# One layer's two seams: the first attention group prepared inside the projection, and the merge's first operands brought in under attention

## The chip, the cores and the metric

One core of a Trainium2 chip runs the whole program. The time is the device time of one execution in microseconds (us); of several runs the median is taken. The engines are TensorE (PE; its weight loads are listed as PEld), VectorE (DVE), ScalarE (ACT), GpSimd (POOL) and SyncE (SP), which here only issues transfers. POOL issues some transfers as well. Sums land in PSUM, whose regions carry names that begin with acc (accA, accS, accT, accO, accX, accC); everything else lies in SBUF.

## The reference

Two layers over 1024 latent tokens and, in the first layer only, 256 context tokens, all of width 1024. Each layer has a mixer (Fourier, global attention, window attention, gated merge) and an expert layer. The change touches the mixer.

```python
def mixer_sublayer(h, hc, cos, sin, w_in, ..., w_out, need_ctx):
    lf, lgq, lgk, lgv, lwq, lwk, lwv, lgate = split_proj(h @ w_in)
    cf, cgq, cgk, cgv, cwq, cwk, cwv, cgate = split_proj(hc @ w_in)
    ...
    o_g = global_attention(q_g, k_g, heads(lgv, G_KV), kc_g, vc_g)    # 8 heads, all keys
    ...
    o_w = window_attention(q_w, k_w, heads(lwv, W_KV), kc_w, vc_w, sink)   # 4 heads, band of 128 each way
    y = gated_merge(lgate, fourier_mix(lf), o_g, o_w,
                    w_br_fourier, w_br_global, w_br_window, w_out)

def gated_merge(gate_cols, f_mix, o_g, o_w, w_br_fourier, w_br_global, w_br_window, w_out):
    g = jax.nn.sigmoid(gate_cols).reshape(gate_cols.shape[:-1] + (N_BRANCH, D_MODEL))
    m = (g[..., 0, :] * (f_mix @ w_br_fourier)
         + g[..., 1, :] * (o_g @ w_br_global)
         + g[..., 2, :] * (o_w @ w_br_window))
    return m @ w_out
```

## The kernel before

Every product that needs full precision is done as three matmuls on a high and a low part of both operands (the helper `mm3`, lines 246 to 248 in the profile). The parts are made by a cast on ACT (line 229, for weights) and a subtraction on DVE (line 233).

A layer's mixer runs in four stages, one behind the other.

- `project` for the context and then for the latents: column blocks 0, 1 and 2 of `w_in`, each over eight tiles of 128 tokens, 24 matmuls of 128x512 a tile. `qtile` takes each finished tile out of PSUM: rotary products on DVE (lines 471 and 473) and POOL (477), the values V copied by ACT into `VT` (545). Block 2 is the last, and its eight tiles give the window heads' queries, keys and values.
- `attention`: 128 queries by four heads make a group. Groups of type 0 (global) have ten key tiles, those of type 1 (banded) four or five, and in the first layer there are groups of context queries with two. `build_k` turns the keys of one type: ten transposes by the identity, casts of the high part, subtractions for the low part. Of each group `prep` transposes the queries, `smax` multiplies the queries by all keys once to find row maxima (12 matmuls into the three banks accS in a group of type 0), `rmax` reduces these on DVE, `mdiag` and `mrow` set the maxima up as a row. Then come the group's steps, one for each key tile: `scores` (two matmuls into accT), the exponential on ACT, and `pv` (into accO) three steps later. `outp` and `recip` write sums to DRAM through SP. The preparation of later groups is spread over the steps of the earlier ones by `pace`; the first group's stands ahead of all steps. All instructions of this stage go through `Pin`, which fixes their order on each engine to the order in which they are written, and all of them carry the line of that helper, 754.
- `merge` in chunks of 512 tokens: `stage` loads the normalised tokens' parts HH and HL (eight transfers on POOL's queue, lines 1072 and 1073), `loads` brings the attention's output in (1078, on SP), multiplies its rows by the reciprocal sums (1095 and 1096) and makes its two parts OH and OL (1097 and 1098). `gates` runs twelve pieces, each two gate products (48 matmuls), a sigmoid (1136) and two branch products. In the first layer the generator `ada`, which makes the modulation rows of both layers, runs along: weights loaded by SP (311), products on ACT (335), sums on POOL (340) and on DVE (342), totals by a cast on ACT (318), a subtraction on DVE (319) and a few matmuls (321 and 322).
- the expert layer, which the change does not touch.

Outside `Pin` the scheduler sets each engine's order. PSUM has two layouts, `cut_main` and `cut_attn`; the projection uses the first, attention the second. SBUF is laid out by hand: `O_K` holds the projected keys, `O_H` first the normalised tokens (`LH`, `LL`) and during attention the turned keys, the number in a name such as a35840 being a place in SBUF.

## Time and profile before

| | us |
|---|---|
| median of 3 runs | 4104.14 |
| the 3 runs | 4103.4 to 4107.11 |
| the profiled execution | 4101.36 |
| its span in the trace | 4099.5 |

| | busy, share of the span |
|---|---|
| TensorE matmuls | 3734.9 us, 91% |
| VectorE | 2813.0 us, 69% |
| ScalarE | 2022.1 us, 49% |
| GpSimd | 682.3 us, 17% |

The tables of stages below give, for a stretch from one time to another (us from the span's start), the busy time of each engine and in brackets the number of its instructions, then the granted TensorE clock (1.00 is 2.4 GHz, 0.50 is 1.2 GHz) and the share and rate of the transfers. In the first layer the projection ends at 261, attention at 667 and the merge's first two pieces at about 733; in the second layer the same three places are 2543, 2929 and 2972.

### The profile page before, as it was taken

To read this page: it belongs to the slowest core of one execution; us is meant where nothing else is said; L and a number is where in the kernel's file an instruction comes from. 1 tells how busy PE (TensorE), PEld (TensorE's weight loads), DVE (VectorE), ACT (ScalarE), POOL (GpSimd) and SP (SyncE) were. 2 spreads that over 40 slices of the span, in tenths; PEclk is the share of its full clock that TensorE was granted. 3 is DMA by queue.
4 is the path that set the end of the run, shared out by engine and by line. 5 is a ranking of instruction groups with operands and counts; after the bars stand their busy time and mean duration, and the time that the engine had idled before them with its cause. 6 is when DMAs were issued, how large, how long until landed. Compare 5 with 4: busy or idle time off the path is not lost.

```text
span 4099.5 us, 52368 instructions
## 1 busy us (share of the span) xinstructions
PE 3734.9 (91%) x19185; PEld 2962.7 (72%) x19185; DVE 2813.0 (69%) x4989; ACT 2022.1 (49%) x3169; POOL 682.3 (17%) x558
## 2 busy tenths in 40 slices
PE   7979998899988698999999888999999994999997
PEld 4756665688788687778888666565588884777775
DVE  5855556957658577877777686555345747899988
ACT  4225555534424365556666541555432331777775
POOL 0240003512302423351000014000000001001000
PEclk9989999999999799999999998999999997999999
DMA  7331004555564477777777642200324434999996
GB/s 246 130 59 56 11 13 145 177 175 192 182 200 160 162 250 260 239 253 251 258 252 247 200 152 42 73 15 10 109 95 162 161 117 170 336 375 376 380 376 239
DMA packets 498542, 749.06 MB, mean 183 GB/s; under 512 B 27088, under 2 KB 291536, under 8 KB 498026
## 3 DMA queue, kind: packets, MB, share of 16 engines
q1 hardware_dynamic: 461164, 654.14, 46.5%
q0 software_dynamic: 31936, 72.70, 7.1%
q10 hardware_dynamic: 5184, 18.88, 1.1%
q8 instruction: 151, 2.47, 0.2%
q14 instruction: 107, 0.88, 0.1%
HBM read 675.21 MB, written 70.52 MB: 182 GB/s over the span
## 4 chain that ended last, share of the span: by engine, by line
PE 55%; DVE 16%; issue 15%; DMA 8%; ACT 3%; POOL 3%; SPq 0%; POOLq 0%; ACTq 0%; DVEq 0%
PE accA L246 11%; PE accA L248 11%; PE accA L247 10%; PE accO L754 8%; PE accT L754 4%; DVE a_r L233 4%; PE accS L754 3%; PE accA L1478 2%; DMA a_f<-in_w_in_dram 2%; POOL a_f L754 2%; PE accA L1476 2%; ACT a_r L229 1%; DVE a_f L342 1%; DMA a_f<-in_w_ada_dram 1%; DMA a_f<-in_w_down_e_dram 1%
## 5 line engine op out<-in xcount | busy, mean ns | idle before, releaser
L233 DVE TENSOR_TENSOR a_r<-a_f,a_r 128x1024 fp32r<-128x1024 f32 (+1 forms) x1008 | 1215.5, 1225 | 419.3 <-ACT a_r L229 396.7
L229 ACT CAST a_r<-a_f 128x1024 fp32r<-128x1024 f32 (+1 forms) x1036 | 1042.0, 1028 | 681.4 <-DVE a_r L233 260.1
L246 PE MATMUL accA<-a_r,a_r 128*128 128x512 f32 (+1 forms) x3280 | 1221.5, 374 | 54.9 <-DVE t L1163 9.2
L247 PE MATMUL accA<-a_r,a_r 128*128 128x512 f32 (+1 forms) x3280 | 1213.8, 371 | 23.2 <-DVE a_r L233 19.0
L248 PE MATMUL accA<-a_r,a_r 128*128 128x512 f32 (+1 forms) x3280 | 1209.8, 370 | 22.1 <-POOL a_r L231 8.5
L246 PEld LDWEIGHTS accA<-a_r,a_r 128*128 128x128 f32 x3280 | 629.4, 192 | 197.9 <-issue 14.2
L248 PEld LDWEIGHTS accA<-a_r,a_r 128*128 128x128 f32 x3280 | 628.5, 192 | 134.1 <-DVE a_r L1375 9.9
L247 PEld LDWEIGHTS accA<-a_r,a_r 128*128 128x128 f32 x3280 | 629.7, 192 | 129.0 <-DVE a_r L233 28.1
L1478 PE MATMUL accA<-a_r,a_r 128*128 128x320 f32 x2048 | 540.9, 316 | 18.1 <-DVE a_f L1486 15.4
L1476 PE MATMUL accA<-a_r,a_r 128*128 128x256 f32 x1792 | 487.3, 284 | 0.0
L754 DVE TENSOR_REDUCE m<-accS 128x1 f32<-128x512 f32 (+2 forms) x536 | 287.3, 560 | 224.0 <-PE accS L754 220.6
L754 PE MATMUL accO<-a_f,a_f 128*65 128x512 f32 (+1 forms) x976 | 416.0, 522 | 0.0
L754 PE MATMUL accT<-a_r,a_r 128*128 128x512 f32 (+1 forms) x976 | 404.0, 508 | 0.0
L754 ACT ACTIVATE a_f<-accT 128x512 f32<-128x512 f32 x408 | 243.7, 598 | 309.6 <-PE accT L754 307.1
L1478 PEld LDWEIGHTS accA<-a_r,a_r 128*128 128x128 f32 x2048 | 375.7, 192 | 21.9 <-DVE a_f L1486 17.1
L1476 PEld LDWEIGHTS accA<-a_r,a_r 128*128 128x128 f32 x1792 | 347.8, 194 | 0.7
L754 PEld LDWEIGHTS accT<-a_r,a_r 128*128 128x128 f32 x976 | 174.7, 191 | 181.2 <-issue 146.4
L754 PE MATMUL accS<-a_r,a_r 128*128 128x512 f32 (+2 forms) x704 | 208.8, 368 | 30.9 <-DVE a_r L754 19.3
L754 PEld LDWEIGHTS accS<-a_r,a_r 128*128 128x128 f32 x704 | 130.2, 202 | 64.3 <-DVE m L754 20.9
L754 PEld LDWEIGHTS accO<-a_f,a_f 128*65 128x65 f32 x976 | 127.0, 137 | 40.7 <-ACT a_f L754 0.3
L340 POOL TENSOR_TENSOR a_f<-a_f,a_f 128x512 f32<-128x512 f32 x84 | 136.0, 1620 | 104.9 <-ACT a_f L335 94.8
L1136 ACT ACTIVATE a_f<-accA 128x512 f32<-128x512 f32 (+1 forms) x120 | 66.2, 553 | 175.2 <-PE accA L248 174.3
(294 smaller groups left out, 3865.0 us busy)
## 6 DMA issues: line engine op xcount, KB each, us to landing
a_f<-in_w_gate_e_dram SPq DMA_DIRECT2D x128, 1024.0 KB
a_f<-in_w_up_e_dram SPq DMA_DIRECT2D x128, 1024.0 KB
a_f<-in_w_down_e_dram SPq DMA_DIRECT2D x128, 1024.0 KB
a_f<-in_w_in_dram SPq DMA_DIRECT2D x60, 1024.0 KB
a_f<-in_w_ada_dram SPq DMA_DIRECT2D x60, 512.0 KB
a_f<-in_w_out_dram SPq DMA_DIRECT2D x20, 1024.0 KB
a_f<-in_w_in_dram SPq DMA_DIRECT2D x36, 512.0 KB
hTd<-a_r SPq DMA_DIRECT2D x8, 2048.0 KB
```

What stands on the lines that cost most here:

```text
L229: S.copy(hi[:, c], raw[:, c])
L233: V.tensor_sub(lo[:, c], raw[:, c], f(hi[:, c]))
L246: PE.matmul(ps, lhsT=lh, rhs=rh, start=start, stop=False)
L247: PE.matmul(ps, lhsT=lh, rhs=rl, start=False, stop=False)
L248: PE.matmul(ps, lhsT=ll, rhs=rh, start=False, stop=stop)
L340: G.tensor_tensor(acc_[0], prod[:, 0] if h == 0 else acc_[0], prod[:, k], op=OP.add)
L342: V.scalar_tensor_tensor(acc_[1], w[:, k], c2[:, kk * h + k, 1:2], zero.to_broadcast([128, 512]) if h + k == 0 else acc_[1], op0=OP.mult, ...
L754: return lambda *a, **k: tc.keep_in_program_order(fn(*a, **k))
L1136: S.activation(sg, gp, AF.Sigmoid)
L1476: PE.matmul(ps[:, 512 * t:512 * t + 256], lhsT=wl[:, k, fc], rhs=xg[:, k, 0:256], start=False, stop=False)
L1478: PE.matmul(ps[:, 512 * t:512 * t + 320], lhsT=wh[:, k, fc], rhs=xg[:, k, 0:320], start=k == 0, stop=k == 7)
```

## The change

It has four parts.

1. The first group's preparation (the keys of type 0, `prep`, the twelve `smax` and their reductions, `mdiag`, `mrow`) becomes a generator `front`, of which `project` runs one step behind each third of a tile's matmuls (one `mm3`) in block 2 from the fifth tile on. For it PSUM is laid out as `cut_attn` ahead of the context's projection, and the projection's tiles go to accO. The keys of type 0 go to the places of token columns whose projection is done.
2. `main` is what is left of attention: the keys of type 1 are built in its steps 1 to 7, the Fourier work runs in odd steps from the ninth, and the banded groups are dealt out over the first six tenths of attention, not over all of it.
3. Six steps behind the last banded group the places of type 1's keys are free, and `stage` of the merge's first chunk is issued there, from POOL. `weights` loads the merge's first two weight pieces some 30 steps ahead of the end and splits them in the last twelve.
4. The merge's SBUF is laid out anew to fit; the sums of `ada` lie in places that attention uses until its end (`O_GB`), the last reciprocals are written behind the merge's first piece.

```diff
-    def project(l, hh, hl, nt, isctx, kvonly, fills=()):
+    def project(l, hh, hl, nt, isctx, kvonly, fills=(), front=None):
...
-                ps = accA()
+                ps = accP()
                 for k in range(8):
                     wh, wl = u[k // 2]
                     mm3(ps[:, 512 - n:512], hh[:, k, 128 * j:128 * j + 128], hl[:, k, 128 * j:128 * j + 128],
                         wh[:, k % 2], wl[:, k % 2], k == 0, k == 7)
+                    if front and blk == 2 and j >= 4:
+                        next(front, None)
...
+        todo = []
+        for t0, t1 in ((2, 6), (6, 10), (0, 2)):
+            n, d = 128 * (t1 - t0), 128 * t0
...
+                for kv in range(2):
+                    hi, a = KT[ty, kv][0](d, n), slice(64 * kv, 64 * kv + 64)
+                    S.copy(hi[0:64], pt[a, :n])
+                    if ty == 0:
+                        V.tensor_copy(hi[64:128], pt[a, :n])
+                    else:
+                        S.copy(hi[64:128], pt[a, :n])
+                for kv in range(2):
+                    a = slice(64 * kv, 64 * kv + 64)
+                    V.tensor_sub(KT[ty, kv][1](d, n)[0:64], pt[a, :n], f(KT[ty, kv][0](d, n)[a]))
+            pt = bank(split)
...
+    RINGS = {"p": [O_H + 512 + 1024 * i for i in range(7)],
+             "es": [O_L + 5120 + 512 * i for i in range(3)], "u": [O_K + 1536, O_K + 2048],
...
-        for off, part in ((0.9, [g for g in gs if len(g["keys"]) == 2]),
-                          (0.8, [g for g in gs if 2 < len(g["keys"]) <= 5]), (0.5, [g for g in gs if len(g["keys"]) > 5])):
...
+        for off, end, part in ((0.9, 1.0, [g for g in gs if len(g["keys"]) == 2]),
+                               (1.3, 0.6, [g for g in gs if 2 < len(g["keys"]) <= 5]),
+                               (0.5, 1.0, [g for g in gs if len(g["keys"]) > 5])):
+            mix += [(end * (k + off) / len(part), len(mix) + k, g) for k, g in enumerate(part)]
...
+        def front():
...
+            bk = build_k(0, V, S, G, PE, sbank)
+            next(bk)
+            prep(g0)
+            yield
+            prep2(g0)
+            next(bk)
+            yield
+            prep3(g0)
+            for _ in bk:
+                yield
+            for u in range(len(units(g0))):
+                smax(g0, u)
+                yield
+                if u:
+                    rmax(g0, u - 1)
+            rmax(g0, u)
+            mdiag(g0)
+            yield
+            yield
+            mrow(g0)
+            yield
+
+        def main(hooks):
...
+            for n in range(len(steps) + 4):
+                if n < len(steps):
+                    scores(*steps[n])
+                for x in first[n] + acts[n]:
+                    x()
+                if 1 <= n <= 7:
+                    next(bk1, None)
...
+                if n > 8 and n % 2 == 1:
+                    next(fill, None)
+                if n == kind1 + 6:
+                    hooks["stage"](G)
+                if n == max(kind1 + 12, len(steps) - 30):
+                    for _ in fill:
+                        pass
+                    ld = hooks["weights"](V, S)
+                    next(ld)
+                if n >= len(steps) - 12:
+                    next(ld, None)
+                if 3 <= n < len(steps) + 3:
+                    pv(*steps[n - 3])
...
+        def weights(V, S):
+
+            ld = [wm.begin(*piece(n), V=V, S=S) for n in range(2)]
+            yield
+            for hi, lo, split in ld:
+                early.append((hi, lo))
+                yield from split
...
-                         [44032 + 512 * i for i in range(4)], act=True)
+                         [O_GB + 512 * i for i in range(4)], act=True)
...
-                hooks[0] = lambda: steps(ld, 99)
+                hooks[0] = lambda: (steps(ld, 99), [x() for x in late])
```

TensorE, first layer, end of the projection, before: the last tile's last three matmuls (accA), and behind them the turning of the keys (ident is the identity, a23552 the projected keys) and the queries' first product with the keys (accS).

```order
L246 MATMUL accA_2227<-a10240_1024_r_483,a30208_8192_r_190 128x512
L247 MATMUL accA_2227<-a11264_1024_r_485,a30208_8192_r_190 128x512
L248 MATMUL accA_2227<-a10240_1024_r_483,a38400_8192_r_191 128x512
L754 MATMUL accT_2287<-ident_79,a23552_2560_f_107 128x128 x4
L754 MATMUL accT_2288<-ident_79,a23552_2560_f_107 128x128 x4
L754 MATMUL accO_2289<-ident_79,a23552_2560_f_107 128x128 x2
L754 MATMUL accX_2283<-ident_79,a12288_6144_f_104 64x128 x4
L754 MATMUL accS_2284<-a30208_1280_r_2315,a26112_512_r_2335 128x512
```

The same work after, in the fifth tile of block 2 (accO_2153 is that tile).

```order
L256 MATMUL accO_2153<-a4096_1024_r_181,a30208_8192_r_206 128x512
L257 MATMUL accO_2153<-a5120_1024_r_183,a30208_8192_r_206 128x512
L258 MATMUL accO_2153<-a4096_1024_r_181,a38400_8192_r_207 128x512
L792 MATMUL accS_2158<-ident_79,a23552_2560_f_107 128x128 x4
L792 MATMUL accX_2157<-ident_79,a12288_6144_f_104 64x128 x4
L256 MATMUL accO_2153<-a4096_1024_r_181,a30208_8192_r_206 128x512
L257 MATMUL accO_2153<-a5120_1024_r_183,a30208_8192_r_206 128x512
L258 MATMUL accO_2153<-a4096_1024_r_181,a38400_8192_r_207 128x512
L792 MATMUL accS_2159<-ident_79,a23552_2560_f_107 128x128 x4
```

The preparation has moved between the tile's own matmuls, and the turned keys land in the three accS banks, which `smax` uses next.

ScalarE, first layer, last exponentials of attention and first work of the merge, before (335 and 318 belong to `ada`, 229 splits a weight, 1085 and 1097 are the merge's `loads`, a28672 is the attention's output as loaded).

```order
L1085 CAST a40960_512_r_4900<-a41472_512_f_3137 6x512
L754 COPY a25600_512_f_2802<-accO_2290 65x512
L229 CAST a9216_3072_r_5061<-a6144_3072_f_5062 128x1024
L335 ACTIVATE a14336_1024_f_4877<-a12288_1024_f_4875,c2_95 128x512 x2
L318 CAST t512_5167<-a44032_512_f_5032 128x512
L229 CAST a9216_3072_r_5061<-a6144_3072_f_5062 128x1024
L335 ACTIVATE a15360_1024_f_4878<-a13312_1024_f_4876,c2_95 128x512 x2
L318 CAST t512_5173<-a44544_512_f_5033 128x512
L229 CAST a9216_3072_r_5061<-a6144_3072_f_5062 128x1024
L1097 CAST a24576_4096_r_4871<-a28672_4096_f_4881 128x512 x2
```

The same place after (348, 331 and 1165 are the lines that were 335, 318 and 1097; a20480 is the attention's output as loaded; a35840 is the sum that POOL makes, and accT_2398 is the last exponential but one).

```order
L792 ACTIVATE a35840_512_f_2507<-accT_2398 128x512
L1153 CAST a32768_512_r_4931<-a33280_512_f_4930 6x512
L792 ACTIVATE a36864_512_f_2524<-accT_2399 128x512
L1153 CAST a32768_512_r_4931<-a33280_512_f_4930 6x512
L792 COPY a25088_512_f_2643<-accO_2400 65x512
L348 ACTIVATE a14336_1024_f_2386<-a12288_1024_f_2384,c2_95 128x512
L792 COPY a25600_512_f_2783<-accO_2401 65x512
L348 ACTIVATE a14336_1024_f_2386<-a12288_1024_f_2384,c2_95 128x512
L348 ACTIVATE a15360_1024_f_2387<-a13312_1024_f_2385,c2_95 128x512 x2
L331 CAST t512_5176<-a35840_512_f_2507 128x512
L1165 CAST a16384_4096_r_2380<-a20480_4096_f_2390 128x512
```

The weight splits are gone from here, and the first cast of the attention's output stands behind the cast of POOL's sum, whose place a35840 the last exponential but one still writes.

TensorE, first layer, the last `pv` and the first gates, before and after (the merge's tokens are a16384 and a20480 before, a38400 and a42496 after).

```order
L754 MATMUL accO_2290<-a11776_512_f_2546,a18432_5120_f_106 65x512
L1095 MATMUL accT_4994<-a40960_512_r_4900,a46080_384_r_112 128x512
L1095 MATMUL accT_4994<-a41472_512_r_4901,a46080_384_r_112 128x512
L1095 MATMUL accT_5000<-a40960_512_r_4900,a46080_384_r_112 128x512
L1095 MATMUL accT_5000<-a41472_512_r_4901,a46080_384_r_112 128x512
L321 MATMUL accC_5166<-t512_5167,e2_96 2x512
L246 MATMUL accA_4925<-a16384_4096_r_4869,a0_2560_r_4914 128x512
```

```order
L792 MATMUL accO_2401<-a36864_512_f_2524,a18432_2640_f_106 65x512
L256 MATMUL accA_4943<-a38400_4096_r_2378,a0_2560_r_4661 128x512
L257 MATMUL accA_4943<-a42496_4096_r_2379,a0_2560_r_4661 128x512
L258 MATMUL accA_4943<-a38400_4096_r_2378,a3072_2560_r_4663 128x512
L256 MATMUL accA_4943<-a38400_4096_r_2378,a0_2560_r_4661 128x512
```

The gates follow the last `pv` directly; the first totals of `ada` and the row factors come later.

## Rows read from the trace of the kernel before

**Rows 1.** The page's chain that ended last: share of the span by engine.

```profile
PE 55%; DVE 16%; issue 15%; DMA 8%; ACT 3%; POOL 3%; SPq 0%; POOLq 0%; ACTq 0%; DVEq 0%
```

**Rows 2.** Busy time by stage, first layer; last come granted clock, transfer share, GB/s.

```profile
240.00:261.00 21.00, 21.00 (x93) 17.08 (x92) 4.00 (x15) 1.07 (x4) 4.63 (x8) 1.00 0.00 1
261.00:286.00 25.00, 14.35 (x57) 10.53 (x57) 16.72 (x36) 8.25 (x17) 13.47 (x24) 0.65 1.06 169
286.00:300.00 14.00, 9.58 (x31) 6.76 (x30) 6.96 (x13) 9.02 (x19) 1.99 (x4) 0.66 0.42 55
300.00:340.00 40.00, 38.80 (x181) 24.98 (x180) 20.96 (x50) 20.95 (x38) 2.91 (x6) 1.00 0.22 66
667.00:733.00 66.00, 47.65 (x157) 31.72 (x157) 56.79 (x61) 34.87 (x54) 38.79 (x30) 0.82 0.63 201
```

**Rows 3.** The same view, second layer: attention's start, then attention's end into the merge.

```profile
2543.00:2568.00 25.00, 14.49 (x55) 10.69 (x56) 16.73 (x36) 8.02 (x17) 13.51 (x24) 0.61 0.91 166
2568.00:2582.00 14.00, 8.60 (x32) 6.24 (x31) 7.22 (x14) 9.25 (x19) 2.32 (x5) 0.72 0.47 61
2929.00:2972.00 43.00, 33.88 (x124) 24.14 (x123) 19.17 (x26) 13.91 (x20) 4.25 (x8) 0.92 0.50 169
```

**Rows 4.** Timeline, first layer, around attention's start: start, duration, instructions, idle before.

```profile
260.67 0.39 PE L248 MATMUL accA<-a_r,a_r 128*128 128x512 f32 x1
...
262.69 1.28 ACT L754 ACT_TABLE_LOAD   x1
...
262.72 1.09 PE L754 MATMUL accT<-ident,a_f 128*128 128x128 f32 x8 [1.67 <-ACT a_f L545]
...
268.12 1.62 DVE L754 TENSOR_REDUCE m<-accS 128x1 f32<-128x512 f32 x3 [0.26 <-PE accS L754]
...
272.05 1.27 DVE L754 TENSOR_TENSOR a_r<-accT,a_r 64x512 fp32r<-64x512 f32 x2
...
285.81 1.20 PE L754 MATMUL accT<-a_r,a_r 128*128 128x512 f32 x2
...
286.10 1.92 ACT L754 CAST a_r<-accS 64x512 fp32r<-64x512 f32 x4
...
293.00 1.65 PE L754 MATMUL accS<-a_r,a_r 128*128 128x256 f32 x6 [4.28 <-DVE a_r L754]
```

**Rows 5.** Timeline, first layer, attention's end and the merge's first two pieces.

```profile
663.82 3.17 PE L754 MATMUL accO<-a_f,a_f 128*65 128x256 f32 x10
...
674.87 1.22 PE L246 MATMUL accA<-a_r,a_r 128*128 128x512 f32 x2
...
696.02 1.14 ACT L318 CAST t<-a_f 128x512 fp32r<-128x512 f32 x2 [5.14 <-POOL a_f L340]
...
700.86 1.29 POOL L340 TENSOR_TENSOR a_f<-a_f 128x512 f32<-128x512 f32 x1 [4.86 <-ACT a_f L335]
...
710.04 7.10 POOL L340 TENSOR_TENSOR a_f<-a_f,a_f 128x512 f32<-128x512 f32 x4 [4.86 <-ACT a_f L335]
```

**Rows 6.** Timeline, second layer, attention's end and the merge's first two pieces.

```profile
2925.51 3.61 PE L754 MATMUL accO<-a_f,a_f 128*65 128x256 f32 x16
...
2934.18 1.22 PE L246 MATMUL accA<-a_r,a_r 128*128 128x512 f32 x2 [1.47 <-DMA a_r<-hTd]
...
2951.50 0.38 SPq L1078 DMA_DIRECT2D a_f<-od  x1
...
2956.18 0.69 DVE L1096 TENSOR_TENSOR a_f<-a_f,accT 128x512 f32<-128x512 f32 x1 [3.13 <-DMA a_f<-od]
```

**Rows 7.** The page's costliest groups: busy us and mean ns of one, idle before.

```profile
L233 DVE TENSOR_TENSOR a_r<-a_f,a_r 128x1024 fp32r<-128x1024 f32 (+1 forms) x1008 | 1215.5, 1225 | 419.3 <-ACT a_r L229 396.7
...
L754 ACT ACTIVATE a_f<-accT 128x512 f32<-128x512 f32 x408 | 243.7, 598 | 309.6 <-PE accT L754 307.1
L340 POOL TENSOR_TENSOR a_f<-a_f,a_f 128x512 f32<-128x512 f32 x84 | 136.0, 1620 | 104.9 <-ACT a_f L335 94.8
```

**Rows 8.** Busy time by stage: a stretch of the routing behind the second layer's merge.

```profile
3433.00:3490.00 57.00, 8.99 (x38) 7.83 (x39) 42.27 (x100) 4.65 (x7) 7.69 (x5) 0.50 0.40 145
```

249 lines of the change are left out of this document (123 added, 126 removed).

## The prediction, written before the changed kernel was run

> **What bounds the kernel now.** I read the page's chain first: TensorE carries 55% of it, VectorE and "issue" most of the rest [rows 1]. So TensorE bounds the program where it is fed, and the question is where it isn't. The tables by stage answer that [rows 2, 3]. In the projection TensorE is busy 21.00 us of 21.00, at 93 matmuls of 0.226 us; in settled attention 38.80 of 40. Between them, from 261 to 286, it is busy 14.35 of 25, and that at a granted clock of 0.65, so the real work is smaller still. The timeline shows why [rows 4]: the projection's last matmul ends at 261.06, the first scores start at 285.81, and between them the first group's preparation goes to and fro between TensorE, ScalarE and VectorE. Layer two repeats it, 14.49 of 25 [rows 3]. The second seam is attention's end. Layer one: 157 matmuls in the 66 us to 733, 157 x 0.226 = 35.5, so some 30 us without work. Layer two: 124 x 0.226 = 28.0 in 43 us, so 15 us without. Everything that the change can win lies in these two seams, about 25 + 25 + 30 + 15 us.
>
> **Seam one, projection to attention, for each layer.** What goes is the whole stretch from 261.06 to 285.81, 24.75 us [rows 4]. What comes back, by the step:
>
> - Its TensorE work now stands among the matmuls of block 2, which had no gap. Fourteen transposes at 1.09 / 8 = 0.136 are 1.9 us; eight products of 512 columns at 0.226 and four of half that are 2.3; the four of `mrow` 0.5. Together **4.7 us**.
> - VectorE in the last four tiles of block 2 had 4.00 us of work in 21 [rows 2]. It gets the second copy of the high part and the low part of the keys, two of 512 in 1.27 us and so for all six parts each some 3.4 us, twice, and four heads' reductions at 1.62 for three, 6.5 us, the query's subtraction, 0.7 [rows 4]: with its own 4.4 this is 18.4 us of 21.7 (96 matmuls). In total it fits, but `smax` finds only three accS banks, each freed by a VectorE instruction that may stand behind rope or keys, and TensorE runs in order, so the projection behind a waiting `smax` stands still. Between 0 (all hidden) and 9 us (all 6.5 us of reductions and two key parts of 1.27 waited out); the order shows the turned keys in the same three banks, so I take **4.5 us**.
> - The first exponential waits for ScalarE's copy of the last V tile and its table load, which ends at 262.69 + 1.28 = 263.97, 2.9 us behind the projection. Ahead of it TensorE has two steps of scores, 0.9 us, since there are two accT banks; after it one exponential of 0.6 [rows 7] must end. **2.4 us**, at least 1.
> - Work that stood in the gap and isn't the first group's must now be done in `main`: fifteen Fourier matmuls of the form at 293.00 (six in 1.65 at half clock, so 0.14 each at full) and ten transposes of the second kind's keys. **3.5 us**.
> - That second kind's casts are all ScalarE's: 1.92 us for four and six parts twice over, 6.2 us in all. Before, they stood in 286 to 300, where TensorE lost 4.28 us on VectorE at once and ran at 0.66 [rows 2, 4]. Now they are spread over steps 1 to 7, where ScalarE also has an exponential of 0.6 a step and the next group's query, about 11 us against 9 us of TensorE's work, in banks which `smax` and Fourier want too. Between 5 us better than before and 6 worse (the clock held at half for twice as long); I take **2 us worse**, since the pinned order makes TensorE wait for each split.
>
> Sum: -24.75 + 4.7 + 4.5 + 2.4 + 3.5 + 2 = **-7.6 us a layer**, -15 for both. With the better ends it is -20, with the worse ends about 0.
>
> **Seam two, layer two.** The gates started at 2934.18, five us behind the last `pv` (2925.51 + 3.61), waiting for HH and HL; now these and the first weights lie ready and the gates follow the last `pv`. What is late next: the attention's output. SyncE issues its first part right behind the last store; the later part issued at 2951.50 reached VectorE at 2956.18, 4.7 us [rows 6]. So with two us for the store ahead of it and a cast and a subtraction behind it, each about the 0.69 of the multiplication there, the first branch can start at some 9 us, and the first piece's 48 gate products last 10.9: hidden. The second piece's rows come from parts two and three, which stand behind a wait of SyncE for the last sums, and each row costs three such instructions, 2.1 us, in a chain of VectorE, ScalarE and VectorE; against 10.9 us of gates that leaves some 4 of the 15 us. **-11 us** (8 to 14).
>
> **Seam two, layer one.** Here `ada` runs along. Its sum on POOL now lies in a35840, which the last exponential but one writes and the last `pv` but one reads, so the seven additions that began long ahead of attention's end can only begin at it. Seven at the mean of 1.62 [rows 7] are 11.3 us; undisturbed at 1.29 [rows 5] 9.0; waiting for loads, as from 700.86 to 717.14, 16.3. ScalarE's order then has the cast of that sum ahead of the attention output's first cast, so the first piece's branch starts some 13 us after the end, against 10.9 us of gates, and needs two rows of 1.3 us: 4 to 8 us stand there. Behind ScalarE's waiting cast are queued all casts of `loads` and the sigmoid's table load, and TensorE waits for these. The second and third totals stand ahead of the second piece's branch. Two units at 11 to 16 us and its own 22 products put that end at 48 to 64 us where it was 66. I take 52: **-14 us** (2 to 20). The eight token transfers moved onto POOL stand behind the Fourier operands there and ahead of the additions, which cannot start earlier anyway; they cost POOL's queue some 5 us in attention, where POOL is busy 2.91 us of 40 [rows 2], so nothing. The two weights' splits, six of 1.2 us on VectorE [rows 7] and about as much on ScalarE, fall into the last twelve steps, where each step leaves both half idle: 1 us, within the bounds.
>
> By the Trainium skill, "SBUF — State Buffer", section "Who interferes with whom", an addition on POOL and a VectorE instruction with two SBUF inputs can't run at once, and the second waits. The trace fits that: the mean addition is 1.62 us and those at 700.86 take 1.29 [rows 5, 7]. Without it the unit would be 9.0 us in place of 11.3 and layer one's gain up to 16.
>
> **The banded groups early.** It changes no amount of work; ScalarE and VectorE are half idle in settled attention [rows 2], so a denser first part has room. Nothing, within 3 us either way.
>
> **Sum.** -15 - 14 - 11 = -40. The profiled execution took 4101.36 us, so 4061; it lies 2.8 under the median of the runs, 4104.14, and runs of the changed kernel will spread the same way, so I predict **4064**.
>
> **Rivals.**
> 1. *The seams close almost wholly.* VectorE's 18.4 of 21.7 us hide, the key splits hide behind steps, `ada` keeps pace: the better ends, -40 - 20 - 14, so some 4030. For it: the total work fits on each engine. Against it: three banks and fixed orders, and TensorE already waits on VectorE beside the same work at 268 [rows 4].
> 2. *The preparation's stalls only move.* Block 2 and the first steps of `main` stall for the worse ends (seam one near 0), and `ada` holds the first layer's merge back to 64 us: -0 - 3 - 10, about 4091. For it: VectorE was busy 16.72 of 25 us in the old gap [rows 2], and this work hasn't become less.
> 3. *Slower: the clock stays at half in attention's start.* At 1.2 GHz each us of attention costs half a us, as TensorE is 97% busy there. Before, the 14 us behind the first scores ran at 0.66 [rows 2], so some 9.5 of them at half. From some 50 us a layer on, the 40 us are used up; at 68 us a layer it is 4064 + 2 x 29 = 4122. For it: the clock was 0.50 for all of 3433 to 3490 [rows 8]. Against it: TensorE was busy for a sixth of that, and from 300 on the clock was full again [rows 2].
> 4. *The early transfers don't land early or the scheduler holds the first gates*: only seam one gains, 4089.
>
> On rival 3 the Trainium skill, "TensorE: Matmul & The Clock Gate", section "HAM oscillation — how this bites in real kernels", says that repeated waits between short bursts put the array back to the low clock each time. At 261 to 286 the trace agrees (0.65); whether steps with waits of 1 to 2 us do it, no row here shows.
>
> **How the numbers follow.** The forecast, a gain of 25 to 58 us, 0.66; rival 1 0.15; rival 2 0.11; rival 3 0.04; rival 4 0.04. The range leaves out half of rival 1's better side, rival 3 and a little of rivals 2 and 4: 4032 to 4091. About 0.2%, 8.2 us, is what a measurement can tell from no change; rivals 2 and 4 reach into that in part. Faster 0.88, same 0.08, slower 0.04.
>
> **What would show it.** Block 2's last four tiles should take about 31 us in place of 21.7, with TensorE waiting on VectorE's reductions and casts; the first scores within 1 us of the last tile; the first steps waiting for ScalarE, then a clock below 1.00 for some 10 to 20 us; settled attention at 97%; the first gate directly behind the last `pv` in both layers; in layer one a wait of ScalarE's line 331 for POOL of 8 to 14 us and the branch behind it. I am wrong in seam one if block 2 shows no waits, or if steps 1 to 10 take over 35 us; wrong in seam two if the first layer's second piece ends before 45 us or after 64 us from the last `pv`.

## The result, and the profile after

The changed kernel took 4137.12 us (median of 4 runs, 4136.02 to 4138.38); the kernel before, run beside it, took 4105.28. The ratio is 1.0078, with an interval of 1.0060 to 1.0095: it is slower. That is 73 us above the forecast and 46 above the range's upper end. The profiled span went from 4099.5 to 4135.6 us.

The span can be cut at four places that both traces have: the first matmul of block 2's fifth tile in each layer, and the end of the last `pv` in each layer. Each number is the difference of two rows of the timeline (before, layer one: 239.13 and 666.99; layer two: 2521.06 and 2929.12; after: 236.35 and 686.61, 2551.82 and 2971.65).

| stretch | before | after | forecast of the difference | difference |
|---|---|---|---|---|
| start to layer one's fifth tile | 239.13 | 236.35 | 0 | -2.8 |
| fifth tile to last `pv`, layer one | 427.86 | 450.26 | -7.6 | **+22.4** |
| last `pv` to layer two's fifth tile | 1854.07 | 1865.21 | -14 | **+11.1** |
| fifth tile to last `pv`, layer two | 408.06 | 419.83 | -7.6 | **+11.8** |
| last `pv`, layer two, to the end | 1170.38 | 1163.95 | -11 | -6.4 |
| sum | 4099.5 | 4135.6 | -40 | +36.1 |

So seam one, which was to gain 15 us, lost 34, and of the four stretches with a forecast only the last won. (The first one lies between 236.0 and 239.2 in all kernels here.) The page's chain hardly tells the two kernels apart; compare [rows 1]:

```profile
PE 57%; DVE 15%; issue 14%; DMA 8%; ACT 4%; POOL 3%; SPq 0%; POOLq 0%; ACTq 0%; DVEq 0%
```

Busy time by stage of the kernel after, with the columns of [rows 2, 3]: block 2's last four tiles, 14 and then 40 us behind the first scores, the first layer's merge; then block 2's last four tiles and the merge of the second layer.

```profile
236.35:283.76 47.41, 32.59 (x128) 25.53 (x127) 20.01 (x45) 5.74 (x13) 8.97 (x16) 0.78 0.09 17
283.60:297.60 14.00, 7.30 (x26) 4.43 (x24) 4.83 (x10) 8.14 (x16) 8.08 (x14) 0.69 1.18 179
297.60:337.60 40.00, 34.71 (x143) 21.47 (x144) 21.01 (x50) 17.85 (x35) 5.96 (x11) 0.89 0.20 47
686.60:752.60 66.00, 49.62 (x171) 34.73 (x170) 47.66 (x53) 31.62 (x49) 36.33 (x25) 0.79 0.51 156
2551.80:2598.80 47.00, 32.23 (x128) 25.03 (x127) 19.91 (x45) 5.75 (x13) 8.99 (x16) 0.78 0.09 17
...
2971.65:3014.65 43.00, 36.81 (x140) 26.59 (x140) 14.94 (x21) 11.74 (x17) 0.00 (x0) 0.92 0.32 97
```

Block 2's last four tiles took 47.41 us, forecast 31, before 21.93. VectorE was busy 20.01 us in them, near the 18.4 that the prediction summed; TensorE stood for 14.8 us all the same. What it stood for, from the table of TensorE's waits in 236 to 284 (engine, tile and line, what it waited for, us in all, times, longest; line 256 is the helper `mm3`, line 792 is `Pin`):

```profile
PE accO L256 <- DVE a_r L792: 7.9, 2, 4.0
PE accO L256 <- DMA a_r<-in_consts_dram: 7.0, 1, 7.0
```

It isn't the queries' product with the keys (accS) that waits, as the prediction had it, but the projection itself (accO, line 256). Its operands are weights and tokens, and neither is made by these instructions. The chain of waits shows what they are: the fill of a block of constants into the second part of the keys, by transfers that POOL issues, and then the four casts of a key part, ScalarE and VectorE in turn, and VectorE's two subtractions.

```profile
239.28 3.00 POOL a_r L792 x5
242.28 2.62 DMA a_r<-in_consts_dram
245.04 0.77 PE accO L256
246.66 0.85 PE accS L792 x4
248.31 0.59 ACT a_r L792
248.92 0.69 DVE a_r L792
249.64 0.59 ACT a_r L792
250.25 0.69 DVE a_r L792
250.98 0.69 DVE a_r L792
251.69 0.70 DVE a_r L792
252.53 0.77 PE accO L256
```

The four casts and the subtractions read one accS bank and none overlaps another. The Trainium skill, "PSUM — Partial Sum Buffer", section "PSUM bank collisions raise a hardware error", says that the compiler's scheduler sets instructions of two engines that touch the same bank and the same quarter of its partitions one behind the other, reads too. The first two casts read the same 64 partitions and agree. The third, at 249.64, reads the other 64 and stands behind the second all the same, so here the order goes by the whole bank.

TensorE's list of instructions, with the semaphores that each waits for, has the reason. The number is the place in the list; DMASW is a transfer that POOL issued, DVE is VectorE, Activation is ScalarE. It could be read ahead of the run:

```
770 L792 MATMUL accX_2157<-ident_79,a12288_6144_f_104 64x128 x4
771 L256 MATMUL accO_2153<-a4096_1024_r_181,a30208_8192_r_206 128x512 [waits DMASW6_49,DMASW7_49,DMASW4_49,DMASW3_49]
772 L257 MATMUL accO_2153<-a5120_1024_r_183,a30208_8192_r_206 128x512
...
778 L256 MATMUL accO_2153<-a6144_1024_r_187,a30208_8192_r_206 128x512 [waits DVE_49,Activation_49]
...
785 L256 MATMUL accO_2153<-a8192_1024_r_511,a30208_8192_r_206 128x512 [waits DVE_49,Activation_49]
```

a30208_8192_r is `LH`, the tokens' high part, declared as one region of 8192 columns. The first group's keys go into columns of it that the projection no longer reads. But the program's order between a write and a later read is kept by the region, not by the column, so the next token matmul waits for each key write that stands ahead of it: at 771 for the four fills that land in these columns, at 778 and 785 for a cast and a subtraction of a key part. That is theory A; the experiments test it.

Behind the first scores, attention itself took 403.01 us in place of 381.18 (layer one) and 373.00 in place of 361.08 (layer two), +21.8 and +11.9 where +7.9 was forecast. Summing the gaps and the work between TensorE's rows: idle time went from 7.1 to 22.1 us and from 11.4 to 16.2, work from 374.1 to 381.0 and from 349.6 to 356.8. TensorE's waits in 284 to 687, layer one:

```profile
PE accS L792 <- DVE a_r L792: 9.7, 4, 3.5
PE accT L792 <- ACT a_f L792: 5.0, 5, 1.9
PE accS L792 <- DVE mrs L792: 3.0, 3, 1.5
PE accS L792 <- ACT a_r L792: 2.4, 2, 2.1
PE accS L792 <- DVE m L792: 2.0, 5, 1.1
```

Of the 22.1 us, 11.7 stand in the first 25 us (TensorE's and the other engines' timeline):

```profile
285.38 1.28 ACT L792 ACT_TABLE_LOAD   x1
...
287.42 0.73 PE L792 MATMUL accT<-a_r 128*128 128x512 f32 x2 [1.85 <-ACT a_f L792]
...
289.17 2.36 ACT L792 CAST a_r<-accS 64x512 fp32r<-64x512 f32 x4
291.56 1.39 DVE L792 TENSOR_TENSOR a_r<-accS,a_r 64x512 fp32r<-64x512 f32 x2 [2.53 <-ACT a_r L792]
...
293.00 0.58 PE L792 MATMUL accS<-a_r,a_r 128*128 128x256 f32 x1 [2.70 <-DVE a_r L792]
```

The second kind's keys hold an accS bank for four casts and two subtractions, 2.36 + 1.39 us, and the next group's first product waits for that bank: 2.70 us here, then 3.50 and 2.52. Before, one such wait of 4.28 stood there [rows 4]. The other part of the loss is in the clock row: 0.89 over 297.60 to 337.60 where it was 1.00 [rows 2], that is 22% of 40 us at half, which costs half of 8.8, some 4 us.

### The profile page after: what moved, and what is told of

Its sections match the earlier page's. It is cut to its first block, busy times and chain, and to the rows that moved or that the text cites. A ratio compares the mean times of both kernels' runs of the same rounds, so it can differ in the third digit from the quotient of the medians.

```text
span 4135.6 us, 52377 instructions
## 1 busy us (share of the span) xinstructions
PE 3744.7 (91%) x19185; PEld 2963.4 (72%) x19185; DVE 2813.3 (68%) x4989; ACT 2019.4 (49%) x3169; POOL 687.4 (17%) x566
## 4 chain that ended last, share of the span: by engine, by line
PE 57%; DVE 15%; issue 14%; DMA 8%; ACT 4%; POOL 3%; SPq 0%; POOLq 0%; ACTq 0%; DVEq 0%
PE accA L256 10%; PE accA L258 10%; PE accA L257 10%; PE accO L792 8%; PE accT L792 4%; DVE a_r L242 4%; PE accS L792 4%; PE accA L1561 2%; DMA a_f<-in_w_in_dram 2%; PE accA L1559 1%; ACT a_r L238 1%; POOL a_f L792 1%; PE accO L256 1%; PE accO L257 1%; DVE a_f L355 1%
## 5 line engine op out<-in xcount | busy, mean ns | idle before, releaser
L238 ACT CAST a_r<-a_f 128x1024 fp32r<-128x1024 f32 (+1 forms) x1024 | 1031.3, 1030 | 679.3 <-DVE a_r L242 258.2
L256 PE MATMUL accA<-a_r,a_r 128*128 128x512 f32 (+1 forms) x2816 | 1040.3, 370 | 38.2 <-ACT a_r L1165 5.6
L258 PE MATMUL accA<-a_r,a_r 128*128 128x512 f32 (+1 forms) x2816 | 1029.9, 367 | 23.6 <-POOL a_r L240 11.0
L257 PE MATMUL accA<-a_r,a_r 128*128 128x512 f32 (+1 forms) x2816 | 1033.0, 367 | 7.1 <-DVE a_f L1164 3.6
L256 PEld LDWEIGHTS accA<-a_r,a_r 128*128 128x128 f32 x2816 | 540.6, 192 | 157.7 <-ACT a_r L1457 8.6
L258 PEld LDWEIGHTS accA<-a_r,a_r 128*128 128x128 f32 x2816 | 540.7, 192 | 116.7 <-POOL a_r L240 12.3
L257 PEld LDWEIGHTS accA<-a_r,a_r 128*128 128x128 f32 x2816 | 541.1, 192 | 93.4 <-DVE a_r L242 7.4
L1561 PE MATMUL accA<-a_r,a_r 128*128 128x320 f32 x2048 | 539.4, 315 | 20.8 <-DVE a_f L1569 18.4
L1561 PEld LDWEIGHTS accA<-a_r,a_r 128*128 128x128 f32 x2048 | 374.2, 191 | 25.4 <-DVE a_f L1569 20.9
L1559 PEld LDWEIGHTS accA<-a_r,a_r 128*128 128x128 f32 x1792 | 346.0, 193 | 0.7
L792 PE MATMUL accT<-a_r 128*128 128x512 f32 x512 | 255.4, 580 | 8.7 <-ACT a_f L792 8.7
L256 PE MATMUL accO<-a_r,a_r 128*128 128x512 f32 (+1 forms) x464 | 189.8, 411 | 43.0 <-DVE a_r L792 15.5
L257 PE MATMUL accO<-a_r,a_r 128*128 128x512 f32 (+1 forms) x464 | 186.3, 403 | 16.0 <-DVE a_r L242 15.7
L792 PEld LDWEIGHTS accT<-a_r 128*128 128x128 f32 x512 | 97.0, 192 | 135.5 <-issue 99.0
L258 PE MATMUL accO<-a_r,a_r 128*128 128x512 f32 (+1 forms) x464 | 184.3, 399 | 0.2 <-DVE a_r L469 0.2
L240 POOL TENSOR_TENSOR a_r<-a_f,a_r 128x1024 fp32r<-128x1024 f32 x28 | 70.5, 2525 | 486.7 <-ACT a_r L238 413.0
```

Of the source, the lines that this page charges most:

```text
L238: S.copy(hi[:, c], raw[:, c])
L240: G.tensor_tensor(lo[:, c], raw[:, c], f(hi[:, c]), op=OP.subtract)
L256: PE.matmul(ps, lhsT=lh, rhs=rh, start=start, stop=False)
L257: PE.matmul(ps, lhsT=lh, rhs=rl, start=False, stop=False)
L258: PE.matmul(ps, lhsT=ll, rhs=rh, start=False, stop=stop)
L792: return lambda *a, **k: tc.keep_in_program_order(fn(*a, **k))
```

## The experiments

Times are medians; each ratio is to the kernel before in the same series, whose median was 4102.9 to 4106.35. The last columns are from the traces, as in the table above: block 2's last four tiles, then attention from the first scores to the last `pv`, layer one / layer two.

| kernel | us | ratio, interval | four tiles | attention |
|---|---|---|---|---|
| before | 4102.9 to 4106.35 | 1 | 21.93 / 21.93 | 381.18 / 361.08 |
| after | 4137.12 | 1.0078, 1.0060 to 1.0095 | 47.41 / 46.99 | 403.01 / 373.00 |
| e1_halves | 4095.94 | 0.9981, 0.9970 to 0.9992 | 27.38 / 27.17 | 402.02 / 373.36 |
| e2_behind | 4124.73 | 1.0045, 1.0030 to 1.0061 | 21.93 / 21.93 | 403.00 / 372.55 |
| e3_ada | 4141.77 | 1.0090, 1.0065 to 1.0116 | 47.43 / 46.82 | 407.76 / 372.96 |
| c1_halves_ada | 4091.22 | 0.9969, 0.9959 to 0.9979 | 27.39 / 27.17 | 407.34 / 373.21 |
| e4_k1bank | 4094.77 | 0.9968, 0.9955 to 0.9981 | 27.37 / 27.18 | 400.38 / 370.06 |
| e5_band | 4114.23 | 1.0020, 1.0010 to 1.0030 | 27.40 / 27.15 | 397.79 / 380.77 |
| e6_noearly | 4093.23 | 0.9971, 0.9962 to 0.9981 | 27.35 / 27.16 | 399.55 / 371.50 |
| e7_parts | 4090.44 | 0.9966, 0.9954 to 0.9978 | 27.37 / 27.16 | 402.23 / 372.21 |
| e8_pace | 4089.21 | 0.9968, 0.9958 to 0.9979 | 27.38 / 27.14 | 406.76 / 372.69 |
| e9_table | 4096.57 | 0.9983, 0.9974 to 0.9993 | not read | not read |
| c2_k1_ada | 4080.92 | 0.9942, 0.9925 to 0.9958 | 27.38 / 27.16 | 404.81 / 369.98 |
| c3_all | 4072.27 | 0.9922, 0.9908 to 0.9935 | 27.38 / 27.15 | 402.99 / 369.09 |

The runs of one kernel lie 7 us apart (e1: 4092.8 to 4100.02) to 17 (e8: 4082.87 to 4100.14), and the kernel before differs by up to 3.5 us from series to series. The series are e1, e2, e3 and c1; e4, e5, e6 and c2; e7, e8, e9 and c3; kernels of two series are better compared by their ratios. Where the intervals of two ratios overlap, as those of e1 with c1, e4, e6, e7, e8 and e9, the totals alone don't tell the kernels apart; the stretches of the traces are read there.

**e1_halves: the tokens' places declared in two halves.**

```diff
-        LH = regr(O_H, 8192).rearrange("p (k n) -> p k n", k=8)
-        LL = regr(O_H + 8192, 8192).rearrange("p (k n) -> p k n", k=8)
+        LH, LL = (Halves(*(regr(o + h, 4096).rearrange("p (k n) -> p k n", k=8) for h in (0, 4096)))
+                  for o in (O_H, O_H + 8192))
...
-    RINGS = {"p": [O_H + 512 + 1024 * i for i in range(7)],
+    RINGS = {"p": [O_H + 4096 + 512 * i for i in range(7)],
```

Tokens 0 to 511 are one region, tokens 512 to 1023 another; the keys go into the first, which the last four tiles don't read, and the exponentials' places in attention (`RINGS`) move along. No work is added or taken.

> Change: the projection's tokens LH and LL are declared in two halves of 512 columns each, so that the keys of type 0 are put into a region that the last four tiles of block 2 do not read; order of instructions as in the changed kernel. Theory A (a matmul of the projection waits for every write into its region, so for the constant fills and the key splits, 7.0 + 3.9 + 3.8 us a layer, and the clock falls to half behind it): block 2's last four tiles shrink from 47 us to 28 to 32, the time falls by 30 to 38 us, to 4099 to 4107. Rival B (VectorE and the three banks are the bound, the wait only moves from the tile's matmuls to the key products): the time falls by 0 to 12 us, 4125 to 4137, and the waits stand before accS matmuls.

Measured: 4095.94, 41 us below the kernel after and 3 below theory A's range, and the four tiles went from 47.41 to 27.38 us. Their row of busy time by stage:

```profile
235.99:263.37 27.38, 27.29 (x128) 21.42 (x127) 19.53 (x45) 5.65 (x13) 9.01 (x16) 1.00 0.16 30
```

TensorE is busy 27.29 of 27.38 us, at the full clock, with the same 128 entries, and the waits at 771, 778 and 785 are gone from its list. Theory A holds: the three waits came from the declared region, and they took the clock down with them (0.78 against 1.00). Of the 20.0 us that the change of declaration gave back, 14.8 were the waits and the rest the clock. What is left, 27.38 - 21.93 = 5.5 us, is TensorE's own work for the first group. Attention did not move (402.02 against 403.01).

One thing more changed. In layer one ScalarE's first cast of the attention output (line 1175 here, at 669.15) now stands ahead of the modulation totals' casts (line 331, at 681.63), and the first 48 gate products end 11.3 us behind the last `pv` in place of 18.4. By the 450th matmul nothing of this is left (138.3 in e1, 134.7 in the kernel after), so nearly all of the 41 us is the four tiles' 20.0 and 19.8.

**e2_behind: the preparation back behind the projection, all else as after.**

```diff
-                    if front and blk == 2 and j >= 4:
-                        next(front, None)
```

> Change: the first group's preparation is run behind the projection, not in it; all else as in the changed kernel. Theory A (inside the projection it costs about 25 us a layer, as much as the old gap): the same time within 8 us, 4129 to 4145. Rival C (the preparation did gain its 8 us a layer in the projection, and the loss lies in attention's first steps alone): slower by 15 us or more, 4152 and up.

Measured: 4124.73, 12 us below the kernel after: 4 below theory A's range and far from rival C's 4152. The four tiles are back at 21.93, and 20.1 us pass from their end to the first scores: 42.0 from the fifth tile to the scores, against 47.3 in the kernel after and 46.7 before. Attention is as long as in the kernel after (403.00 / 372.55). So inside the projection the preparation cost 5 us a layer more than behind it, and what lengthens attention isn't where the first group is prepared. What is left for that is the work moved into the steps behind it and the new order of the groups.

**e4_k1bank: the second kind's keys turned in a bank of accO, on top of e1.**

```diff
-            bk1 = build_k(1, V, S, G, PE, sbank)
+            bk1 = build_k(1, V, S, G, PE, lambda r: OB[1], True)
```

It runs in steps 0 to 6, one key part at a time.

> On top of e1_halves: the keys of type 1 are turned in the second accO bank, which the first group does not use yet, part by part in steps 0 to 5, and not in the three accS banks. Theory F (attention's first steps lose time because the key products of the next group wait for a bank that the split of these keys holds, 2.70 + 3.50 + 2.52 us a layer, and the half clock behind it): attention from the first scores to the last pv shrinks by 5 to 10 us a layer, the time by 10 to 18, to 4078 to 4086. Rival G (ScalarE's casts themselves bind the first steps, whichever bank they read): within 4 us of e1_halves, 4092 to 4100.

Measured: attention 1.6 and 3.3 us shorter than in e1, where theory F had 5 to 10; the total lies in rival G's range, and its ratio, 0.9968 against 0.9981, has an interval that overlaps e1's. Of the first steps' gaps in layer one, 2.70, 3.50 and 2.52 us became 2.69, 2.09 and 1.89. The first is a wait for a bank still, now that of accO: the next key part's turning waits for the split of the one before.

```profile
271.47 2.35 ACT L806 CAST a_r<-accO 64x512 fp32r<-64x512 f32 x4
273.85 1.39 DVE L806 TENSOR_TENSOR a_r<-accO,a_r 64x512 fp32r<-64x512 f32 x2 [2.05 <-ACT a_r L806]
275.39 1.09 PE L806 MATMUL accO<-ident,a_f 128*128 128x128 f32 x4 [2.69 <-DVE a_r L806]
```

The others are waits for the maxima `m`. So which bank it is was a part only: the split of a key part takes ScalarE some 2.36 and VectorE 1.39 us one behind the other, wherever it lies, and what is next on that bank and on these engines waits for it.

**e9_table: the exponential's table loaded in block 2, on top of e1.**

```diff
+            S.activation(junk, sink8[:, 0:1], AF.Exp)
```

It stands in `front`, ahead of `mrow`, and not at the start of `main`.

> The two halves, and the small exp that loads ScalarE's table stands at the start of the run in block two instead of behind the max rows. Theory: the first exp after the scores waits for the table (a gap of 1.85 us on TensorE before accT in the trace of after, layer two), so with the table loaded under the projection the gap goes to about 0.5 and both layers win 1 to 2 us: total 2 to 4 less than the halves kernel, 4092 to 4094. Rival: ScalarE's casts of block two reload a table of their own behind it, and the first exp pays again: no change, 4094 to 4098. Second rival: what waits next on the first steps (VectorE's key products for a bank, 2.5 to 3.5 us gaps) takes the gain: no change in the last pv either.

Measured: 4096.57 against 4095.94, no change. The stretches are read in c3_all, which has the same edit and e4's: its table load begins at 256.86, ahead of the first scores at 265.16, and the first steps of layer one read (TensorE):

```profile
267.49 0.73 PE L806 MATMUL accT<-a_r 128*128 128x512 f32 x2 [0.36 <-ACT a_f L806]
...
272.68 1.09 PE L806 MATMUL accO<-ident,a_f 128*128 128x128 f32 x4 [2.70 <-DVE a_r L806]
```

The wait for the table fell from 1.85 to 0.36 us, and the long wait behind it is as long as in e4 (2.69 there). Whether the 1.5 us reach the end can't be told from the totals.

**e5_band: the banded groups dealt over all of attention again, on top of e1.** The tokens' places then come free late, so their loads are issued at attention's end (two more lines of the edit do this, left out here); the weights still come early.

```diff
-                               (1.3, 0.6, [g for g in gs if 2 < len(g["keys"]) <= 5]),
+                               (1.3, 1.0, [g for g in gs if 2 < len(g["keys"]) <= 5]),
```

> On top of e1_halves: the banded groups dealt out over the whole attention again, so that the tokens for the merge can only be loaded at attention's end; the weights stay early. Theory H (dealing the banded groups out over six tenths overloads the reductions and ScalarE there: the single waits of 1 to 2 us near 349, 357, 426 and 588 in layer one): attention from the first scores to the last pv shrinks by 4 to 8 us in layer one and 0 to 3 in layer two, given back at the merges' start: 4090 to 4100. Rival I (the order of groups costs nothing): attention as long as in e1_halves, the merges' starts 3 to 6 us later, 4100 to 4108.

Measured: 4114.23, 18 us above e1 (16 by the ratios) and above both ranges. In layer one attention is 4.2 us shorter (the waits for `mrs` are gone), in layer two 7.4 longer, for which no run here gives the cause, and the first piece's 48 gate products end 25.0 and 20.3 us behind the last `pv`, against 11.3 and 12.4. They wait for the tokens, as the timeline of TensorE in layer one shows:

```profile
665.28 0.70 PE L256 MATMUL accA<-a_r,a_r 128*128 128x512 f32 x2 [1.56 <-DMA a_r<-hTd]
672.38 0.76 PE L257 MATMUL accA<-a_r,a_r 128*128 128x512 f32 x1 [6.40 <-DMA a_r<-hTd]
```

So the early banded groups are what lets seam two close. In layer one they cost 4 us of attention; on the whole they pay.

**e6_noearly: no loads written into attention, on top of e1.** The calls for the tokens and the first weights stand behind attention in the code, the banded groups early as in the change.

```diff
-                if n == kind1 + 6:
-                    hooks["stage"](G)
...
-        late = attn({"stage": ahead, "weights": chunks[0][7]})
+        late = attn({})
...
         cut_main()
+        ahead(G)
```

> On top of e1_halves: the merge's tokens and first weights are loaded behind attention and not in it; layout and order of groups as in the changed kernel. Price of the early loads, with the modulation sums left as in the changed kernel. Theory J (in layer one the merge follows the modulation sums from the sixth piece on, so the early loads are worth nothing there, and only layer two's 5 us count): 5 to 9 us slower than e1_halves, 4101 to 4105. Rival K (they are worth their 11 to 14 us in each layer, as forecast): 4117 and up.

Measured: 4093.23, the same as e1 and below both ranges, and the first 48 gate products end 11.2 and 11.8 us behind the last `pv`, as soon as with the written order. In layer one the tokens' first load goes out 111.0 us ahead of the last `pv`, in e1 113.5 ahead: the scheduler moves these loads up by itself once their places are free. Of the change's third part only the free places do the work.

**e7_parts: all parts of the attention's output asked for at once, on top of e1.**

```diff
-            part(0, 2)
+            for k in (0, 2, 5):
+                part(k, min(k + 3, 8) if k else 2)
...
-                if k in (2, 5):
-                    part(k, k + 3)
```

> The two halves of the first kernel of this series (the split places declared in two halves), and in both layers all three parts of the attention output's load issued at the start of `loads`, before the output projection's first pieces, instead of parts two and three inside the pieces' loop. Theory: in layer one part two goes out late (2987.3 us in the trace of after, 15.7 us behind the last pv, part three 27.3 us behind it) because its place is declared as one with the first piece's raw loads, so it waits for that piece's last read, and SyncE stands there. With the parts issued first they wait for nothing but the attention's own sums: the 200th matmul behind layer one's last pv comes 3 to 5 us earlier than the 56.9 us of the halves kernel, layer two (places free in the same way) up to 3 earlier, total 3 to 8 us less than the halves kernel (4095.9), 4088 to 4093. Rival: SyncE waits for the attention's last sums, as the prediction had it; then nothing moves, 4094 to 4098. Second rival: the pieces' loads now stand behind the parts in SyncE's queue and the first weights come late: 4099 or more.

Measured: 4090.44, 5.5 us below e1. Layer two's 200th matmul behind the last `pv` comes at 50.9 us (before 62.2, after 56.8, e1 56.9), the 400th at 96.2 (107.6, 102.1, 102.2). In the kernel after, SyncE's timeline has parts two and three 15.7 and 27.3 us behind layer two's last `pv` (2971.65; the expectation gives these numbers to layer one), and its waits in 2965 to 3005 name the reason:

```profile
2987.31 0.38 SPq L1146 DMA_DIRECT2D a_f<-od  x1
...
2998.92 0.37 SPq L1146 DMA_DIRECT2D a_f<-od  x1
```

```profile
SPq L1146 <- DVE a_r L1166: 12.3, 2, 10.0
SPq L1146 <- PE accA L258: 7.1, 1, 7.1
```

Line 1166 makes OL of the first piece, and the output's raw rows lie in the region declared for it. With the parts asked for first (last `pv` at 2928.75):

```profile
2928.78 0.37 SPq L1156 DMA_DIRECT2D a_f<-od  x1
...
2930.31 0.60 SPq L1156 DMA_DIRECT2D a_f<-od  x1
...
2932.92 0.42 SPq L1156 DMA_DIRECT2D a_f<-od  x1
```

TensorE then has 0.3 us of waits in 2928.7 to 2990 where it had 6.2 in the same 62 us of the kernel after. In layer two the theory holds, with 6.0 us; the rival, SyncE waiting for the last sums, falls. In layer one the 200th matmul comes only 2.1 us earlier than in e1 (62.1 against 64.2), and at the 400th nothing is left (119.0 against 116.4).

**e3_ada, c1_halves_ada and e8_pace: the modulation.** e3 gives the first of `ada`'s units places of its own in the kernel after, so that it can run inside attention; c1 does that on top of e1; e8 also thins the first chunk's hooks from four pieces of modulation to three.

```diff
-                         [O_GB + 512 * i for i in range(4)], act=True)
-                     for u in (todo[:8], todo[8:], [])]
+                         a_, act=True)
+                     for u, a_ in ((todo[:8], [O_CQ, O_CQ + 512] + ([O_GB + 512 * i for i in (2, 3, 0, 1)] * 4)[:14]),
+                                   (todo[8:], [O_GB + 512 * i for i in range(4)]), ([], [0]))]
```

```diff
-                at(n, lambda f_=fill, k=4 if i < 2 else 2: steps(f_, k))
+                at(n, lambda f_=fill, k=(3, 4, 2)[i]: steps(f_, k))
```

> Change: the first unit of the modulation sums gets two places that attention leaves free (28672 and 29184), the other units the places of the changed kernel in another turn. Theory D (the merge of layer one follows the modulation sums, whose first total moved from 674 to 695 us and whose last from 842 to 862, because their place is taken until the last pv): the totals come some 20 us earlier against the last pv, the time falls by 10 to 20 us, 4117 to 4127. Rival E (the merge is bound by its own pieces there): 4133 to 4138.

> Change: both of the above, halves of the tokens' region and free places for the first modulation unit. Theories A and D: the gains add, 40 to 55 us, 4082 to 4097, faster than the kernel before (4105). With B and E: 4120 to 4137.

> The two halves with the first modulation unit at its own place (4091.2 us), and the hooks of layer two's first chunk take three modulation pieces at a time instead of four. Theory: merge's first layer follows the modulation's end (its pieces stand in VectorE's and ScalarE's rows ahead of the gate's), so a thinner front gives the projection's start its casts earlier: the 300th matmul behind the last pv 3 to 6 us earlier than the 82.9 us, total 4084 to 4090. Rival: the modulation is a fixed amount of work on the two engines and only its place changes; the 1000th matmul stays at 240, total 4089 to 4094. Second rival: the unit's end comes later and the stage that reads it waits: 4097 or more.

Measured, in us from layer one's last `pv` to the end of its nth matmul:

| n | before | after | e1 | c1 | e8 | c3 |
|---|---|---|---|---|---|---|
| 48 | 22.2 | 18.4 | 11.3 | 11.9 | 11.9 | 10.9 |
| 157 (two pieces) | 65.7 | 63.2 | 54.5 | 49.8 | 51.2 | 43.9 |
| 400 | 125.4 | 119.8 | 116.4 | 106.6 | 107.1 | 105.0 |
| 450 | 136.8 | 134.7 | 138.3 | 126.5 | 118.4 | 123.6 |
| 600 | 174.6 | 175.8 | 175.9 | 166.2 | 152.5 | 165.3 |
| 1000 | 247.7 | 251.3 | 249.5 | 240.0 | 238.7 | 238.0 |

In e1 the merge is 11 us ahead of the kernel before at the 157th matmul, 9 at the 400th and 1.5 behind at the 450th. What ends the lead is VectorE. By stage, around the 400th to the 450th matmul of e1:

```profile
757.50:781.60 24.10, 24.10 (x107) 19.24 (x106) 19.41 (x21) 9.12 (x14) 11.73 (x8) 1.00 0.44 140
781.60:803.50 21.90, 15.95 (x52) 11.21 (x51) 20.74 (x22) 13.51 (x21) 13.15 (x8) 0.77 0.56 178
```

VectorE is busy 20.74 us of 21.90, TensorE 15.95, and the clock falls. TensorE waits there for VectorE's part of a modulation total and for its weight subtractions:

```profile
PE accC L335 <- DVE t L332: 3.7, 2, 2.0
PE accA L258 <- DVE a_r L242: 2.2, 2, 1.8
```

The modulation's sums are VectorE's costliest group in the 72 us up to there (e1, 731 to 803.5):

```profile
L355 DVE SCALAR_TENSOR_TENSOR a_f<-a_f,c,a_f 128x512 f32<-128x512 f32 x23 | 24.3, 1056 | 3.8 <-DMA a_f<-in_w_ada_dram 3.5
```

The kernel before in the same part of the merge, its third piece on:

```profile
733.00:841.60 108.60, 102.55 (x444) 81.24 (x445) 93.12 (x95) 52.28 (x78) 50.37 (x30) 1.00 0.59 192
```

VectorE had 15 us to spare in 109; a merge that starts earlier brings its own work onto VectorE before the modulation is through. With the first unit inside attention (c1) the merge keeps 9.5 us on e1 at the 1000th matmul, but attention is 5.3 us longer, and the total is 4.7 lower. In e3 the two cancel: 4141.77, above both ranges and no better than the kernel after. e8 shows a third form: 13.7 us ahead of c1 at the 600th matmul, 1.3 at the 1000th, where the work put off is done. Its rival is right, and its total, 4089.21, is c1's within noise.

**c2_k1_ada and c3_all: together.** c2 is e1, e4 and the modulation's places; c3 adds e7 and e9.

> On top of e4_k1bank: the free places for the first modulation unit of e3_ada. With theory F and the 4.7 us that these places brought on top of e1_halves: 4073 to 4082. With rival G: 4088 to 4095.

> All edits that should gain together: the two halves, the type-one keys turned in a bank of their own, the modulation unit at its own place (these three measured 4080.9), the parts of the attention output first, and the table under the projection. If the last two are worth what the theories say the total is 5 to 10 us less than 4080.9, 4071 to 4076; if their rivals hold, 4078 to 4084, the same as without them.

Measured: 4080.92 and 4072.27, each in the range of its theories. c3 beats the kernel before by 0.78% (interval 0.65 to 0.92%) and the kernel after by 65 us. Its merge's starts, by stage, against [rows 2, 3]:

```profile
668.15:734.15 66.00, 62.51 (x256) 46.73 (x256) 57.45 (x65) 33.75 (x52) 33.88 (x20) 0.97 0.57 181
2919.63:2962.63 43.00, 42.69 (x168) 32.12 (x167) 17.83 (x26) 12.83 (x19) 0.00 (x0) 0.92 0.37 120
```

256 matmuls in the 66 us that held 157, and 168 in the 43 that held 124.

## Why the prediction was wrong, by its own steps

**Seam one, what goes: right.** The 24.75 us between projection and first scores (25.05 in layer two) are gone in both layers: 283.60 is directly behind the last tile.

**Seam one, TensorE's work in block 2: right.** 4.7 forecast, 5.5 and 5.2 measured with the waits taken away (e1).

**Seam one, VectorE and the three banks: the step that failed.** The prediction asked which engine could be too slow and which bank could be held, put 4.5 us on it with 0 to 9 as ends, and named `smax` as the instruction that waits. The cost was 47.41 - 27.38 = 20 us a layer, and not by that mechanism: the banks alone cost nothing that e1 shows, where TensorE stands for 0.09 us in 27.38. The region's waits held the projection, and the clock fell behind them. These 40 us for two layers are the largest of the terms that missed; attention's first steps and the rest of it add 18, layer one's merge 25, layer two's 5, and what came out better takes 11 off: 76 us between forecast and span. The bound was wrong because the step reasoned from amounts of work. The instructions' order was read for what stands where, and not for what each waits for, although the list with the waits shows three new ones on matmuls that the change doesn't touch. The row at 268 to which rival 1 points shows VectorE waiting for TensorE; TensorE's own waits for the maxima in that gap, 4.1 us in the trace of before, did not come along into block 2.

**Seam one, the first steps of attention: mechanism right, size off.** 2.4 + 3.5 + 2 = 7.9 was forecast, +21.8 and +11.9 measured. Three things make the difference. The work and the clock cost 6.9 and 7.2 us where 3.5 and a part of the 2 stood. The waits of the first 50 us rose by 6.4 and 5.3 (5.5 to 11.9, 6.8 to 12.1), mostly the second kind's splits, which were put at 2 with an end at 6 worse. And in layer one 8.6 us of small waits are spread over the rest. Some 3 of them are gone where the banded groups are dealt late (e5, 6.4 us of waits behind the first 50 against 9.3 in e1), which the prediction put at nothing within 3; the cause of the others is open. With the region's waits out of the way, layer two's seam one gives 400.38 - 408.06 = -7.7 us, the forecast's -7.6; but it does so because 5.2 in place of 9.2 in block 2 makes up for 12.3 in place of 7.9 in attention. That number was right for the wrong reasons.

**Seam two, layer two: direction right, size halved, cause misnamed.** -11 forecast, -5.4 at the 200th matmul. The gates did follow the last `pv` directly (2971.08). The parts two and three were said to stand behind the last sums; they stood behind the first piece's reads of one declared region, the same mechanism as in block 2. With that out (e7) the gain is 62.2 - 50.9 = 11.3.

**Seam two, layer one: the local steps right, the end wrong.** POOL's seven additions began at attention's end (685.84) and took 9.4 us, between the forecast's 9.0 and 11.3. ScalarE's rows:

```profile
695.31 0.62 ACT L331 CAST t<-a_f 128x512 fp32r<-128x512 f32 x1 [4.68 <-POOL a_f L353]
695.84 0.61 ACT L1165 CAST a_r<-a_f 128x512 fp32r<-128x512 f32 x1
```

The attention output's cast stood behind the total's, and TensorE waited 4.41 us for it (4 to 8 forecast). The second piece ended at 63.2 us, where 52 was taken and 64 was the worst end. What the prediction left out is the stretch behind it: it stopped at the second piece and took its gain as won. There VectorE, filled by the modulation and the weight splits, takes the lead back by the 450th matmul of e1 and by the 500th or so of the kernel after, and 6.0 us more are lost between the 3000th and the 4000th, in the routing, which the change doesn't touch (the last section). For another 2.7 us behind the 4000th no run gives a cause.

**Rivals.** Rival 2 had the shape (stalls that only move) but ended at 4091, since it took the worst VectorE case as the worst case. Rival 3 ended on the right side by the wrong means: behind the first scores the clock cost some 4 us a layer, where that rival needed over 25. Slower had a chance of 0.04, as its only mechanism was the clock; a wait that comes from how places are declared was no rival at all.

## What to carry to other kernels

When a dead part of a live tile is used again, declare the live and the dead part as regions of their own, and compare the waits of the instructions that the change does not touch: here the three new waits there cost 20 us a layer, and the work that was moved 5.5. A gain ahead of a stage counts only as far as the next thing that keeps its own pace; ask, some hundreds of instructions on, what ends last there. And a sum that comes out right may hold two wrong terms: judge each term by its own stretch.
